# A two-layer hybrid attention trunk: the order of its instructions taken from the scheduler of the language and made by a recorder in the kernel

## The chip, the core and the metric

The kernel runs on one NeuronCore of a Trainium2 chip. Five engines each work through an instruction stream of their own, in order: PE (matmul), DVE (vector), ACT (scalar), POOL and SP, which here issues every DMA. They wait for each other by semaphores. The metric is the device time of one execution in microseconds (us), and the median over several executions is compared.

## What is computed

`x` is (1, 1024, 1024) float32, and two layers are applied to it. In the reference, cut to what matters:

```python
def hybrid_layer(x, ...):
    h = rms_norm(x, g_pre)
    a_q, a_kv, a_g, b_cq, b_ckv, b_kr, c_q, c_kv, z = split_cols(h @ w_in)
    o_a = nsa_attention(...)            # 4 heads: compressed + selected + window 512, sigmoid gates
    o_b = causal_block_attention(...)   # 4 heads: latent attention, rotary key
    o_c = banded_attention(...)         # 8 heads: window 128, with sinks
    mixed = concatenate([o_a, o_b, o_c], -1) * silu(z)
    return x + rms_norm(mixed @ w_out, g_post)
```

With 1024 tokens there are 16 blocks of 64 and the top 16 are selected, so the selected branch is full causal attention. Heads A and C add a bias by distance.

## The kernel before

Tokens are worked in 8 tiles of 128 (`NT`, index `qt`). To keep float32 precision, every operand of a large matmul is held as two float16 parts, high and low: `split` makes them with one ACT copy and one DVE operation, and a product is three float16 matmuls. Each of the two layers has four stretches:

- `first`: norm of `x` (layer 0 only; later norms are in the stretch before), values by token (`by_token`, line 293), keys and queries (`project`, line 286), and the compression of keys (`compress`, `compress_hidden`). `bias_setup` works out the bias rows once, writes them to DRAM, and replicates them there by four DMAs into `bias_rows_a` and eight into `bias_rows_c`.
- swa: `run(swa_units(L), second(L, l), ...)`, the window-128 heads, with the rest of the projections as filler.
- nsa: `run(nsa_units(L), gate_path(L, l), ...)`, the A heads, with the gate columns (`gate_columns`, line 293 for its matmuls) as filler.
- mla: `last_phase`, the B heads, the output product (`product`, line 932), and the norm that starts the next layer.

Attention goes by units (one branch, one or two heads, one `qt`), each in three steps:

- `score`: PE matmuls into a PSUM bank `psS` (lines 639, 654, 679), a DVE operation that adds the bias and takes the row's minimum (`ttr`, line 597), and the exponential on ACT (`expo`, line 600).
- `turn`: the probabilities are split and transposed. Small units do it on PE (line 718, bank `psT`). Units with `by_dma` set (the larger ones of swa and of nsa, and six tiles of the last mla) split into a staging buffer (`sz`, `KC`, `stage_slc`, `stage_win`) and transpose by a DMA that SP issues (`turn_by_dma`, line 167).
- `values`: 64-column PE matmuls with the transposed probabilities into the bank `psO` (line 730).

`mixed` gates and splits a finished tile and transposes it by DMA out of a `ringS` buffer; `product` then multiplies by `w_out`.

`run` writes the steps interleaved by hand, with a lag of 2 units for `turn` and 4 for `values`, and fillers between them:

```python
for i in range(n + lag_v):
    if i < n:
        units[i].score()
    if 0 <= i - lag_t < n:
        units[i - lag_t].turn()
    if 0 <= i - lag_v < n:
        units[i - lag_v].values()
    while more and spent < total * done / whole:
        w = next(filler, None)
```

That is the order in which the program is written. The order on each engine is then made by the scheduler of the language: it takes a tile's slot from a pool with a number of buffers (`bufs`; `ringS` has 3, PSUM has 3 `psS`, 2 `psT`, 1 `psO`, 2 `psJ`), and lists the instructions with a timing model of its own. Weights come in halves into `ringS` (`load_next`), always three loads ahead of their use.

Of the kernel before, what the change touches and what calls it, by code (L numbers as in the profile page):

```python
# [2 lines left out]

# [9 lines left out]
F32 = mybir.dt.float32  # L13
AF = mybir.ActivationFunctionType
# [72 lines left out]
    return (np.arange(128) >= 31).astype(np.float32).reshape(128, 1)  # L87


@with_exitstack  # L90
def trunk(ctx, tc, a, out):
    nc = tc.nc
    pool = ctx.enter_context(tc.tile_pool(name="sb", bufs=1))
    psum = ctx.enter_context(tc.tile_pool(name="ps", bufs=1, space=bass.MemoryType.PSUM))
    uid = [0]
# [16 lines left out]
    BUFS = {"S": 3, "T": 2, "O": 1, "J": 2}  # L112

    def ps(tag):
        uid[0] += 1
        return psum.tile([128, 512], F32, tag=tag, name=f"ps{tag}_{uid[0]}", bufs=BUFS[tag])

    def split(src, scale, hi, lo):
        nc.scalar.activation(hi, src, AF.Copy, scale=scale)  # L119
# [5 lines left out]
    class Ring:  # L125
# [25 lines left out]
    ident = sb([128, 128], F32, "ident")  # L151
    make_identity(nc, ident)
# [627 lines left out]
    def run(units, filler, total, lag_t, lag_v):  # L780

        whole = sum(u.weight for u in units) or 1
        done = spent = 0.0
        more = True
        n = len(units)
# [3 lines that stand above are left out]
                done += units[i].weight  # L789
# [6 lines that stand above are left out]
                more = w is not None  # L796
                spent += w or 0
        for _ in filler:
            pass

    def swa_units(L):
        r = []
        part = sb([128, D], F32, "sz", 2)

        def hl(u):
            return part[:, 256 * (u.h % 4):256 * (u.h % 4) + 512]

        rings = Ring(arena, 2048, 2560), Ring(arena, 4608, 2560), hl
        for hg in (0, 4):
            for qt in range(NT):  # L810
                g = {}
                r.append(Unit(L, "swa", qt, hg, g, None, rings))
                r.append(Unit(L, "swa", qt, hg + 2, g, "swa", rings))
        return r

    def nsa_units(L):
        r = []
        parts = {"slc": [sb([128, D], F32, "sz", 2), sb([128, D], F32, "stage_slc")],
                 "win": [sb([128, D], F32, "KC"), sb([128, 640], F32, "stage_win")]}
# [170 lines left out]
    for l in range(DEPTH):  # L990
        L = Layer()
        L.hT = hT
        first(L, l, wv)
        run(swa_units(L), second(L, l), 80.0, 2, 4)
        third(L, l)
        run(nsa_units(L), gate_path(L, l), 75.0, 2, 4)
        hT, wv = last_phase(L, l, a["x"] if l == 0 else x1_d, x1_d if l < DEPTH - 1 else out)


def lay_out(inp):  # L1000
# [62 lines left out]
```

## Time and profile before

| what | value |
|---|---|
| three timed runs | 1167.44 us median (1163.13 to 1167.81) |
| the profiled execution's own time | 1160.39 us |
| its span in the profile | 1158.5 us |
| mean granted PE clock | 0.973 |
| PE busy | 1010.7 us (87%) |
| DVE, ACT busy | 759.7 us (66%), 706.5 us (61%) |
| DMA queue, share of 16 DMA engines | 64.3% |

The four stretches of layer 0 end at about 117, 240, 435 and 597 us, those of layer 1 at 697, 805, 1000 and 1158 us. In a row of the profile, the idle time is that of the engine just before the rows' instructions, with what ended most of it. "PE busy" counts a matmul until its modelled end, so two matmuls in a row overlap in it.

### The profile page before, as it was taken

The page shows a single profiled execution, that of the slowest core. Times are in us where ns is not written, and L with a number is a line of the kernel's source. Part 1 is how long each engine was busy: PE and PEld are TensorE (multiplying, and loading weights), DVE is VectorE, ACT ScalarE, POOL GpSimd, SP SyncE. Part 2 cuts the span into 40 slices and gives each one's busy share as a digit, 9 for nine tenths or more (in the row PEclk, how much of TensorE's full clock was granted, in tenths as well). Part 3 has the DMA queues.
Part 4 walks back from the last instruction along what each step waited for, and adds up shares of the span by engine and source line. Part 5 has one row for each costly group of instructions (what it writes and reads, how often), then busy time and mean ns, then how long its engine had stood idle before and what let it go on. Part 6 is the DMA issues. An engine that isn't in the chain of part 4 may idle for free.

```text
span 1158.5 us, 25304 instructions
## 1 busy us (share of the span) xinstructions
PE 1010.7 (87%) x9536; PEld 664.0 (57%) x9536; DVE 759.7 (66%) x2268; ACT 706.5 (61%) x1659; POOL 111.0 (10%) x198
## 2 busy tenths in 40 slices
PE   6979898989988877898979989898998887788977
PEld 4634657658776664455646455664776665534443
DVE  6453677756787766687755346876486776756762
ACT  6451676647777677677634246765586666777651
POOL 1000100001111011211000010000011110121010
PEclk9889999999999998999989999999999999989999
DMA  6685476673688695555476435847437877678893
GB/s 241 154 261 138 115 144 117 129 175 100 128 166 162 132 228 157 152 118 129 97 183 203 115 83 120 169 85 178 131 97 145 175 138 134 197 162 196 180 192 98
DMA packets 313499, 174.43 MB, mean 151 GB/s; under 512 B 273580, under 2 KB 289324, under 8 KB 313376
## 3 DMA queue, kind: packets, MB, share of 16 engines
q1 hardware_dynamic: 313376, 172.81, 64.3%
q8 instruction: 75, 1.23, 0.4%
q14 instruction: 48, 0.39, 0.1%
HBM read 76.63 MB, written 21.41 MB: 85 GB/s over the span
## 4 chain that ended last, share of the span: by engine, by line
PE 28%; DMA 16%; DVE 7%; ACT 6%; issue 3%; POOL 1%; SPq 1%; POOLq 0%; ACTq 0%; DVEq 0%
PE psJ L932 9%; PE psJ L286 8%; PE psJ L293 4%; DMA arena<-sz 3%; PE psO L730 3%; PE psS L679 2%; DMA arena<-ringS 2%; DMA V<-ringS 2%; DMA sz<-gate_rows 2%; DVE arena L597 2%; DMA arena<-stage_slc 2%; DMA arena<-stage_win 2%; PE psT L718 2%; ACT arena L600 1%; DVE sz L120 1%
## 5 line engine op out<-in xcount | busy, mean ns | idle before, releaser
L600 ACT ACTIVATE arena<-arena,mx 128x256 f32<-128x256 f32 (+8 forms) x384 | 226.9, 592 | 118.5 <-DVE mx L597 116.1
L293 PE MATMUL psJ<-W,HT 128*128 128x256 f16 x1920 | 241.5, 273 | 0.8 <-DVE VB L120 0.8
L293 PEld LDWEIGHTS <-HT 128*128 128x128 f16 x2304 | 215.2, 99 | 32.0 <-issue 6.6
L286 PE MATMUL psJ<-HT,W 128*128 128x512 f16 x864 | 199.5, 385 | 15.3 <-DVE R L120 7.6
L730 PEld LDWEIGHTS <-arena 128*128 128x128 f16 x2964 | 120.4, 99 | 77.1 <-DMA arena<-sz 20.2
L286 PEld LDWEIGHTS <-W 128*128 128x128 f16 x864 | 84.1, 99 | 110.0 <-issue 10.7
L730 PE MATMUL psO<-V,arena 128*128 128x64 f16 x2304 | 104.4, 194 | 44.7 <-DMA arena<-sz 17.1
L597 DVE CUSTOM_DVE_ANT_0 arena<-psS,R 128x64 f32<-128x64 f32 (+4 forms) x192 | 86.0, 463 | 45.2 <-PE psS L679 19.6
L679 PE MATMUL psS<-KA,QA 128*128 128x512 f16 (+3 forms) x384 | 78.3, 312 | 1.5 <-DVE mx L597 1.2
L120 DVE SCALAR_TENSOR_TENSOR sz<-arena,sz 128x512 f16<-128x512 f32 (+4 forms) x76 | 57.6, 759 | 24.0 <-ACT sz L119 24.0
L600 ACT ACTIVATION_READ_ACCUMULATOR arena<-arena,mx 128x1 f32 x384 | 72.4, 189 | 0.0
L597 DVE CUSTOM_DVE_ANT_0 arena<-psS,arena,nsink 128x256 f32<-128x256 f32 (+1 forms) x128 | 58.4, 460 | 20.5 <-PE psS L654 20.4
L932 PEld LDWEIGHTS <-arena 128*128 128x128 f16 x384 | 37.2, 101 | 56.4 <-DMA arena<-ringS 13.1
L932 PEld LDWEIGHTS <-V 128*128 128x128 f16 x384 | 36.8, 100 | 54.0 <-DMA V<-ringS 11.5
L120 DVE SCALAR_TENSOR_TENSOR arena<-psT,arena 128x128 f16<-128x128 f32 (+3 forms) x144 | 59.6, 429 | 11.3 <-ACT arena L119 10.6
L120 DVE SCALAR_TENSOR_TENSOR W<-ringS,W 128x1024 f16<-128x1024 f32 x48 | 58.3, 1221 | 11.4 <-ACT W L119 10.7
L718 PE MATMUL psT<-ident,arena 128*128 128x128 f32 x300 | 55.8, 286 | 10.8 <-ACT arena L600 9.7
L119 ACT ACTIVATE arena<-psT 128x128 f16<-128x128 f32 (+3 forms) x144 | 51.8, 383 | 20.2 <-PE psT L718 19.6
L171 POOL TENSOR_TENSOR rs<-rs,halfneg 128x1 f32<-128x1 f32 x48 | 26.3, 548 | 384.9 <-DVE rs L170 274.2
L679 PE MATMUL psS<-KB,QB 96*128 96x512 f16 (+3 forms) x288 | 60.5, 337 | 2.5 <-DVE mx L597 2.4
L932 PE MATMUL psJ<-R,arena 128*128 128x512 f16 x192 | 49.8, 414 | 10.5 <-DMA arena<-ringS 10.5
L119 ACT ACTIVATE sz<-arena 128x512 f16<-128x512 f32 (+4 forms) x76 | 51.8, 682 | 9.1 <-DMA arena<-sz 8.0
(156 smaller groups left out, 1644.1 us busy)
## 6 DMA issues: line engine op xcount, KB each, us to landing
ringS<-in_w_in_dram SPq DMA_DIRECT2D x40, 512.0 KB, 4.7
gate_rows<-sz SPq DMA_DIRECT2D x32, 256.0 KB, 3.8
ringS<-in_w_out_dram SPq DMA_DIRECT2D x16, 512.0 KB, 4.4
sz<-gate_rows SPq DMA_DIRECT2D x16, 512.0 KB, 4.7
R<-in_x_dram SPq DMA_DIRECT2D x8, 512.0 KB, 4.1
ringS<-in_cmp_w_dram SPq DMA_DIRECT2D x8, 512.0 KB, 5.3
x<-in_rope_dram SPq DMA_DIRECT2D x8, 512.0 KB, 6.0
x<-in_x_dram SPq DMA_DIRECT2D x8, 512.0 KB, 4.4
```

Source lines behind the costliest of these rows:

```text
L119: nc.scalar.activation(hi, src, AF.Copy, scale=scale)
L120: nc.vector.scalar_tensor_tensor(lo, src, scale, hi, op0=OP.mult, op1=OP.subtract)
L171: nc.gpsimd.tensor_tensor(dst, dst, half_neg[:, :n], op=OP.pow)
L286: nc.tensor.matmul(p, w[:, x, k, sub * 128:(sub + 1) * 128], L.hT[:, y, k, c * 512:(c + 1) * 512], start=(k == 0 and i == 0), stop=(k == K ...
L293: nc.tensor.matmul(p, L.hT[:, y, k, t * 128:(t + 1) * 128], w[:, x, k, :width], start=(k == 0 and i == 0), stop=(k == KT - 1 and i == 2))
L597: nc.vector.tensor_tensor_reduce(o, i0, i1, -alpha, init, OP.add, OP.min, acc)
L600: nc.scalar.activation(b, b, AF.Exp, bias=mx, scale=-1.0, accum_out=sm)
L679: nc.tensor.matmul(p[:, :n], q, k[:, k0 * 128:k1 * 128], start=(i == 0), stop=(i == len(pairs) - 1))
L718: nc.tensor.transpose(p[:, i * 128:(i + 1) * 128], u.b[:, (g + i) * 128:(g + i + 1) * 128], ident)
L730: nc.tensor.matmul(g["O"][:, key * 64:(key + 1) * 64], u.pt[:, x, i, :], v[:, y], start=(key not in seen and j == 0), stop=(last[key] == n ...
L932: nc.tensor.matmul(p, g["mt"][:, x, k], wo[k // 2][:, w, k % 2, cs], start=(k == 0 and i == 0), stop=(k == KT - 1 and i == 2))
```

## The change

The kernel's source up to the end of the layer loop stays as it is, but `nc` in it is now a `Recorder`. Tiles become `Room`s without an address, accesses become `View`s that know which bytes they touch, and each call becomes a `Step` with the set of steps that it must follow. After the loop the kernel makes one fixed tile for every slot, runs a list schedule, and emits the steps in that order inside `tc.manual_schedule()`, which keeps each engine's order as it is emitted. The number of slots of each tag is the one it had. The core of the diff:

```diff
+    def cost(self, s):
+        ...
+        if s.engine == "tensor":
+            n *= 2 if s.name == "transpose" else 4 if src.dtype == F32 else 1
+            return n / 2.4 + 2.2, n / 2.4 + 200.0
+        wake = 35.0
+        if s.engine == "scalar":
+            t = (160.0 if bank else 205.0) + 0.83 * n + (85.0 if s.args[2] == AF.Exp else 0.0)
+            ...
+        if s.engine == "vector":
+            t = 152.0 + 1.045 * n
+            ...
+            return t - 80.0, t + wake
+        ...
+        if s.name == "dma_start_transpose":
+            return 1300.0, (400.0 + size / 220.0, 2000.0)
+        return 520.0, (size / 200.0, 1900.0)
+
+    def schedule(self, slots):
+        ...
+        for s in reversed(self.steps):
+            ...
+            s.key = -tail[s] if s.engine == "sync" else s.n
+        ...
+        while True:
+            for e, heap in ready.items():
+                if heap and free[e] <= now:
+                    _, _, s = heapq.heappop(heap)
+                    order.append(s)
+                    ...
+                    busy, seen = self.cost(s)
+                    if e == "scalar" and s.args[2] not in (AF.Copy, AF.Square, table[0]):
+                        table[0] = s.args[2]
+                        busy, seen = busy + 1283.0, seen + 1283.0
+                    if e == "sync":
+                        bus[0] = max(bus[0], now + busy) + seen[0]
+                        seen = bus[0] + seen[1] - now
...
 def trunk(ctx, tc, a, out):
-    nc = tc.nc
+    nc = Recorder(tc.nc)
...
     def sb(shape, dtype, tag, bufs=1):
-        uid[0] += 1
-        return pool.tile(shape, dtype, tag=tag, name=f"{tag}_{uid[0]}", bufs=bufs)
+        assert count.setdefault(tag, bufs) == bufs
+        words = math.prod(shape[1:]) * (4 if dtype == F32 else 2) // 4
+        return nc.room(tag, words).view(shape, dtype)
...
+    for tag, words in slots.items():
+        home, n = (psum, BUFS[tag[2:]]) if tag[:2] == "ps" and tag[2:] in BUFS else (pool, count[tag])
+        slots[tag] = [home.tile([128, words], F32, tag=f"{tag}_{i}", name=f"{tag}_{i}", bufs=1) for i in range(n)]
+    order = nc.schedule(slots)
+    with tc.manual_schedule():
+        nc.emit(order)
```

`cost` gives for a step, in ns, how long its engine is taken and when its result is seen. On every engine the earliest written step that is ready goes first (`s.n`); only on SP the step with the longest chain behind it goes first (`tail`). All DMAs share one modelled bus. Instructions are neither added nor taken away, but for the loads of ACT's tables: 39 before and 35 now.

Three places show how instructions move. In the changed kernel all rows carry the line of the emitter (359), and names are those of slots. The first place is PE in the nsa stretch of layer 1, at the selected-branch unit of tile 6 (three score matmul rows shown: two of `psS` are its second bank, of 384 columns). `QA` are queries, `KA` keys, `V` values, `W` gate weights, `HT` the transposed norm. Before:

```order
L679 MATMUL psS_12431<-KA_8037,QA_10009 128x512
L679 LDWEIGHTS QA_10009
L679 MATMUL psS_12434<-KA_8037,QA_10009 128x384
L679 LDWEIGHTS QA_10009
L679 MATMUL psS_12434<-KA_8037,QA_10009 128x384
L730 LDWEIGHTS arena_61
L730 MATMUL psO_12272<-V_7730,arena_61 128x64
```

The same scores of the same unit now:

```order
L359 MATMUL psS_88<-KA_90,QA_126 128x512
L359 LDWEIGHTS QA_126
L359 MATMUL psS_87<-KA_90,QA_126 128x384
L359 LDWEIGHTS QA_126
L359 MATMUL psS_87<-KA_90,QA_126 128x384
L359 LDWEIGHTS HT_71
L359 MATMUL psJ_96<-W_97,HT_71 128x256
```

Behind the scores stood values of an earlier unit (15 matmuls), and now stand four matmuls of gate columns, with those values later. Counted on to this unit's own first values matmul, 122 matmuls stood between before (48 of them of 256 columns, gate columns), and 244 stand between now (96 of 256 columns). The second place is SP's stream where the bias rows are replicated and the compression weights (`cmp_w1`, shown as `in_cmp_w_dram`) are loaded, in layer 0. Before:

```order
L123 DMA ringS_315<-in_cmp_w_dram 128x1024
L123 DMA bias_rows<-arena_61 12x1024
L123 DMA bias_rows<-arena_61 12x733
L123 DMA bias_rows_a<-bias_rows 128x1406 x4
L123 DMA bias_rows_c<-bias_rows 128x383 x8
L123 DMA ringS_548<-in_cmp_w_dram 128x1024
L123 DMA ringS_552<-in_cmp_w_dram 128x1024
```

And in the changed kernel:

```order
L359 DMA ringS_82<-in_cmp_w_dram 128x1024
L359 DMA ringS_83<-in_cmp_w_dram 128x1024
L359 DMA bias_rows<-arena_66 12x1024
L359 DMA x_73<-in_rope_dram 128x1024
L359 DMA ringS_84<-in_cmp_w_dram 128x1024
L359 DMA ringS_82<-in_cmp_w_dram 128x1024
L359 DMA bias_rows_c<-bias_rows 128x383 x2
```

All four halves of these weights now go ahead of the replication, where three of them stood behind it. The third place is SP's first instructions, the loads of `x` and of the first norm's gain (`in_norm_pre_dram`). Before:

```order
L123 DMA R_8_74<-in_x_dram 128x1024
L123 DMA arena_61<-in_norm_pre_dram 128x1024
L123 DMA R_8_74<-in_x_dram 128x1024
L123 DMA ringS_99<-in_w_v_dram 128x816
L123 DMA R_8_74<-in_x_dram 128x1024
```

And in the changed kernel:

```order
L359 DMA R_0_72<-in_x_dram 128x1024 x4
L359 DMA arena_66<-in_norm_pre_dram 128x1024
L359 DMA ringS_84<-in_w_in_dram 128x1024
L359 DMA arena_66<-in_buckets_dram 33x1024
L359 DMA relT_86<-in_relT_dram 32x12
```

The gain now stands behind four tiles of `x`, where it stood behind one.

More of the change, by code (lines that the diff above doesn't have):

```diff
@@ L1 @@
+import heapq
+import itertools
 import math
+import re
 from contextlib import ExitStack
@@ L87, in row_mask, with __init__, then, __getitem__ @@
     return (np.arange(128) >= 31).astype(np.float32).reshape(128, 1)
+class View:
+    def __init__(self, tile, steps, p, ids, dtype):
+        self.tile, self.steps, self.p, self.ids, self.dtype = tile, steps, p, ids, dtype
+        self.shape = (p[1] - p[0],) + ids.shape
+    def then(self, step, p=None, ids=None, dtype=None):
+        return View(self.tile, self.steps + (step,), p or self.p, self.ids if ids is None else ids, dtype or self.dtype)
+    def __getitem__(self, key):
+        key = key if isinstance(key, tuple) else (key,)
+        a, b, _ = key[0].indices(self.shape[0])
+        return self.then(("__getitem__", (key,), {}), (self.p[0] + a, self.p[0] + b), self.ids[key[1:]])
+    def bitcast(self, dtype):
+        ids = self.ids
+        if dtype != self.dtype:
+            ids = ids[..., ::2] if dtype == F32 else np.stack([ids, ids + 1], axis=-1).reshape(ids.shape[:-1] + (-1,))
+        return self.then(("bitcast", (dtype,), {}), ids=ids, dtype=dtype)
+    def rearrange(self, text, **sizes):
+        left, right = [re.findall(r"\([^)]*\)|\w+", s) for s in text.split("->")]
+        names, shape = [], []
+        for word, n in zip(left[1:], self.ids.shape):
+            group = word.strip("()").split()
+            known = math.prod(sizes[g] for g in group if g in sizes)
+            names += group
+            shape += [sizes[g] if g in sizes else n if len(group) == 1 else n // known for g in group]
+        to = [word.strip("()").split() for word in right[1:]]
+        flat = [names.index(g) for group in to for g in group]
+        ids = self.ids.reshape(shape).transpose(flat)
+        ids = ids.reshape([math.prod(shape[names.index(g)] for g in group) for group in to])
+        return self.then(("rearrange", (text,), sizes), ids=ids)
+    def unsqueeze(self, d):
+        return self.then(("unsqueeze", (d,), {}), ids=np.expand_dims(self.ids, d - 1))
+    def to_broadcast(self, shape):
+        return self.then(("to_broadcast", (shape,), {}), ids=np.broadcast_to(self.ids, shape[1:]))
+    def region(self):
+        if self.tile.bank:
+            return 0, 128, 1
+        bits = np.zeros(self.tile.words, np.uint8)
+        bits[self.ids.reshape(-1) // 2] = 1
+        return self.p[0], self.p[1], int.from_bytes(np.packbits(bits).tobytes(), "big")
+    def real(self):
+        v = self.tile.slot
+        for name, args, kwargs in self.steps:
+            v = getattr(v, name)(*args, **kwargs)
+        return v
@@ new lines, with __init__, view @@
+class Room:
+    def __init__(self, tag, words, bank):
+        self.tag, self.words, self.bank, self.users, self.slot, self.left = tag, words, bank, [], None, 0
+    def view(self, shape, dtype):
+        n = math.prod(shape[1:])
+        v = View(self, (), (0, 128), np.arange(self.words) * 2, F32)
+        v = v[:shape[0], :n if dtype == F32 else n // 2]
+        if dtype != F32:
+            v = v.bitcast(dtype)
+        if len(shape) > 2:
+            names = "abcd"[:len(shape) - 1]
+            v = v.rearrange(f"p ({' '.join(names)}) -> p {' '.join(names)}", **dict(zip(names, shape[1:])))
+        return v
@@ L90, in trunk @@
 @with_exitstack
 def trunk(ctx, tc, a, out):
-    nc = tc.nc
+    nc = Recorder(tc.nc)
     pool = ctx.enter_context(tc.tile_pool(name="sb", bufs=1))
     psum = ctx.enter_context(tc.tile_pool(name="ps", bufs=1, space=bass.MemoryType.PSUM))
-    uid = [0]
+    count = {}
     def sb(shape, dtype, tag, bufs=1):
-        uid[0] += 1
-        return pool.tile(shape, dtype, tag=tag, name=f"{tag}_{uid[0]}", bufs=bufs)
+        assert count.setdefault(tag, bufs) == bufs
+        words = math.prod(shape[1:]) * (4 if dtype == F32 else 2) // 4
+        return nc.room(tag, words).view(shape, dtype)
@@ L114, in ps @@
     def ps(tag):
-        uid[0] += 1
-        return psum.tile([128, 512], F32, tag=tag, name=f"ps{tag}_{uid[0]}", bufs=BUFS[tag])
+        return nc.room("ps" + tag, 512, bank=True).view([128, 512], F32)
     def split(src, scale, hi, lo):
@@ L148, in trunk @@
     HL = ((0, 0), (0, 1), (1, 0))
-    ident = sb([128, 128], F32, "ident")
-    make_identity(nc, ident)
+    ident = pool.tile([128, 128], F32, tag="ident", name="ident", bufs=1)
+    make_identity(tc.nc, ident)
     half_neg = sb([128, 8], F32, "halfneg")
@@ L997, in trunk @@
         hT, wv = last_phase(L, l, a["x"] if l == 0 else x1_d, x1_d if l < DEPTH - 1 else out)
+    slots = {}
+    for r in nc.rooms:
+        slots[r.tag] = max(slots.get(r.tag, 0), r.words)
+    for tag, words in slots.items():
[4 more added lines that the diff above has]
+        nc.emit(order)
 def lay_out(inp):
```

141 lines of the change are left out of this document (added).

## The prediction

> **What bounds the kernel now.** I read the page first, then busy time by stretch, then the groups of PE's instructions with what they waited for, and at last the order of time around the waits.
>
> ```profile
> span 1158.5 us, 25304 instructions
> PE 1010.7 (87%) x9536; PEld 664.0 (57%) x9536; DVE 759.7 (66%) x2268; ACT 706.5 (61%) x1659; POOL 111.0 (10%) x198
> ```
>
> PE is busiest, and still idle for 148 us (1158.5 less 1010.7). No other engine is near full, so the time is PE's work plus what PE waits for. By stretch (columns: stretch, busy time of each engine, granted clock, share of the DMA engines, GB/s):
>
> ```profile
> 0.00:117.00 117.00, 97.26 (x614) 55.85 (x615) 56.41 (x106) 51.24 (x90) 5.09 (x14) 0.94 0.68 197
> 117.00:240.00 123.00, 112.61 (x1115) 77.43 (x1114) 94.12 (x324) 86.26 (x259) 8.76 (x16) 1.00 0.63 131
> 240.00:435.00 195.00, 171.42 (x2081) 133.09 (x2079) 136.83 (x455) 130.80 (x339) 23.62 (x50) 0.99 0.71 155
> 435.00:597.00 162.00, 142.37 (x1061) 78.78 (x1059) 112.37 (x288) 104.42 (x182) 21.18 (x28) 0.94 0.55 137
> 597.00:697.00 100.00, 90.11 (x762) 57.51 (x760) 49.94 (x119) 41.88 (x94) 4.93 (x9) 1.00 0.49 137
> 697.00:805.00 108.00, 97.92 (x900) 64.37 (x898) 82.32 (x278) 73.20 (x217) 4.93 (x9) 1.00 0.63 135
> 805.00:1000.00 195.00, 168.26 (x2046) 130.27 (x2046) 132.18 (x439) 128.03 (x332) 24.04 (x50) 0.99 0.69 143
> 1000.00:1158.00 158.00, 130.70 (x971) 66.67 (x968) 95.55 (x263) 90.68 (x151) 18.43 (x22) 0.94 0.72 168
> ```
>
> PE's idle time is spread: 20, 10, 24, 20, 10, 10, 27 and 27 us. So there is no single hole to close; what matters is which waits repeat. The groups of PE that waited most (busy, mean ns | idle before, by releaser):
>
> ```profile
> L730 PE MATMUL psO<-V,arena 128*128 128x64 f16 x2304 | 104.4, 194 | 44.7 <-DMA arena<-sz 17.1 <-DMA arena<-stage_slc 13.6 <-DMA arena<-stage_win 10.2
> L286 PE MATMUL psJ<-HT,W 128*128 128x512 f16 x864 | 199.5, 385 | 15.3 <-DVE R L120 7.6 <-DVE tmp L335 5.3 <-ACT hid L384 1.4
> L718 PE MATMUL psT<-ident,arena 128*128 128x128 f32 x300 | 55.8, 286 | 10.8 <-ACT arena L600 9.7 <-DVE arena L120 0.8
> L932 PE MATMUL psJ<-R,arena 128*128 128x512 f16 x192 | 49.8, 414 | 10.5 <-DMA arena<-ringS 10.5
> L932 PE MATMUL psJ<-R,V 128*128 128x512 f16 x192 | 46.7, 395 | 8.5 <-DMA V<-ringS 8.4
> L654 PE MATMUL psS<-KC,QC 128*128 128x256 f16 x224 | 42.3, 272 | 6.9 <-DVE mx L597 4.6 <-DVE QC L748 1.9
> ```
>
> The first row is the largest: 44.7 us in which PE stands at values matmuls whose transposing DMA has not landed. The other five hold 52.0 us together.
>
> **The change, part by part.** No computation is added or taken away; only places in the streams change.
>
> *A. Values later (nsa).* The unit of the first place shown above, in the order of time:
>
> ```profile
> 934.62 0.92 PE L679 MATMUL psS<-KA,QA 128*128 128x512 f16 x4
> 935.51 0.61 PE L730 MATMUL psO<-V,arena 128*128 128x64 f16 x15
> 935.96 2.79 PE L293 MATMUL psJ<-W,HT 128*128 128x256 f16 x24
> ...
> 936.71 0.48 DVE L597 CUSTOM_DVE_ANT_0 arena<-psS,R,mx 128x256 f32<-128x256 f32 x1
> 938.31 1.04 ACT L600 ACTIVATE arena<-arena,mx 128x896 f32<-128x896 f32 x1 [2.62 <-DVE mx L597]
> 939.62 0.94 ACT L119 ACTIVATE stage_slc<-arena 128x896 f16<-128x896 f32 x1
> 940.93 1.09 DVE L120 SCALAR_TENSOR_TENSOR stage_slc<-arena,stage_slc 128x896 f16<-128x896 f32 x1
> 942.10 2.65 SPq L167 DMA_TRANSPOSE arena<-stage_slc  x1
> 947.38 0.79 PE L730 MATMUL psO<-V,arena 128*128 128x64 f16 x21 [2.02 <-DMA arena<-stage_slc]
> ```
>
> The chain from the last score to the landed transpose takes 947.38 − 935.51 = 11.9 us. The 122 matmuls that PE had to do meanwhile covered 9.9 us of it (all but this wait of 2.0). Now 244 stand there, in a similar mix (48 of 256 columns became 96), so the cover is about 9.9 × 244 / 122 = 19.8 us, 7.9 us more than the chain needs. Over the 80 DMA-transposed nsa units the matmul columns that stand between grow 1.8-fold on average, counted in the order. I expect nine tenths of the 44.7 us to go: −40. Ends: −45, and −15 if the chain grows with the pace (first rival). The waits one by one (total, times, longest):
>
> ```profile
> PE psO L730 <- DMA arena<-sz: 17.1, 16, 3.1
> PE psO L730 <- DMA arena<-stage_slc: 13.6, 12, 2.3
> PE psO L730 <- DMA arena<-stage_win: 10.2, 10, 2.6
> ```
>
> *A'. The tail of each ended wait.* A stall also shows as busy time: the last matmul before it counts its full latency.
>
> ```profile
> 983.79 0.87 PE psO L730 x24
> 949.36 2.62 PE psJ L293 x24
> ```
>
> A 64-column matmul in a row costs 0.87/24 = 36 ns, and the group's mean is 194 ns, so each stall hides some 0.16 us. With the 38 waits above that is −6, between 0 and −7.
>
> *B. The start.* SP's second place:
>
> ```profile
> 42.82 12.18 SPq L123 DMA_DIRECT2D bias_rows_c<-bias_rows  x8
> ...
> 57.59 2.06 SPq L123 DMA_DIRECT2D ringS<-in_cmp_w_dram  x2
> ...
> 65.06 1.06 ACT L119 ACTIVATE arena<-ringS 128x1024 f16<-128x1024 f32 x1 [6.66 <-DMA ringS<-in_cmp_w_dram]
> ...
> 69.72 6.84 PE L286 MATMUL psJ<-HT,W 128*128 128x512 f16 x24 [7.43 <-DVE R L120]
> ```
>
> Eight replications hold SP for 12.2 us, the compression weights go out behind them, ACT waits 6.7 us for them, and the splits that free PE's banks come behind ACT's: PE stands 7.4 us. With the weights ahead that wait goes: −7, and the next thing late is the weights of the group behind, which I leave at nothing since they too go out earlier than the last replications. Against it stands the third place: the norm's gain behind three more tiles of `x`.
>
> ```profile
> R<-in_x_dram SPq DMA_DIRECT2D x8, 512.0 KB, 4.1
> ```
>
> Three more tiles are 1.57 MB; at the 197 GB/s of the first stretch this is 8 us later for the first norm. But the four tiles are then there, and DVE and ACT are half idle in that stretch (56 and 51 of 117 us), so part is caught up: +3, between 0 and +8. Together −4.
>
> *C. The clock.* Behind a long stop of PE the granted clock is halved for a while:
>
> ```profile
> 60.00:75.00 15.00, 7.57 (x29) 2.98 (x28) 7.41 (x12) 7.26 (x12) 0.00 (x0) 0.77 0.85 263
> 441.00:452.00 11.00, 7.91 (x30) 3.16 (x31) 7.06 (x23) 8.53 (x13) 1.95 (x2) 0.53 0.79 229
> ```
>
> In the first, 0.23 × 15 = 3.5 us of clock are lost, about half of them while PE works; that stop is B's, so −2. The second belongs to the entry into mla, which I leave. The nsa stretches run at 0.99 in spite of A's waits, so A brings nothing here. The Trainium skill ("TensorE: Matmul & The Clock Gate", Part 1) says that it takes about 3.4 us of idle array to fall to half clock; the trace agrees, since the longest of A's waits is 3.1 us and its stretches keep the clock, and by that rule too C stays small.
>
> *D. Products (L932), 19.0 us.* In the order as many matmuls stand between the last values of a tile and its first product as before, in most places; in the last layer two products are split and interleaved with values. I take 0, between −10 and +12.
>
> *E. Transposes on PE (L718), 10.8 us.* They wait for exponentials, some of them behind a load of ACT's table. The loads go from 39 to 35: −3, between 0 and −10.
>
> *F. The rest.* Scores waiting for a free bank (L654) and like short waits come from DVE being late by under 1 us; about half of such waits can be filled: −5, between 0 and −10.
>
> Sum: −40 − 6 − 4 − 2 + 0 − 3 − 5 = −60. Against the profiled execution's own 1160.4 us this is 1100. That execution lies 7 us under the median of the timed runs (1167.4) and below the fastest of them (1163.1), so for a median I add half of that: 1103.
>
> **The rivals.**
>
> *The DMA queue becomes the bound of nsa.* Where the DMA transposes are dense:
>
> ```profile
> 319.00:435.00 116.00, 97.95 (x1291) 78.06 (x1288) 86.47 (x274) 82.46 (x179) 14.90 (x29) 1.00 0.83 173
> 870.00:1015.00 145.00, 115.94 (x1481) 89.43 (x1478) 103.64 (x330) 98.28 (x213) 18.23 (x34) 0.99 0.78 158
> HBM read 76.63 MB, written 21.41 MB: 85 GB/s over the span
> ```
>
> The DMA engines work 0.83 × 116 = 96 us and 0.78 × 145 = 113 us there. If PE ran without a wait (98 and 116 us), their share would be 0.98 and 0.97, and transposes would queue. For it speaks that share; against it, that the cover has 7.9 us to spare. If only a third of A and A' comes, it is 1103 + 31 = 1134. The Trainium skill ("Perfetto Trace Analysis", Identifying the Most-Contended Engine) calls occupancy of the 16 DMA engines misleading and would judge by HBM utilization instead, whose row here, 85 GB/s, is far from the 358 GB/s that it gives for a core; by that rule this rival would have half its chance. No run yet tells which measure holds for transposes inside SBUF.
>
> *The waits move to the next engine.* With values later, scores run further ahead, and PE could stop at `psS` banks that DVE has not emptied; DVE works 137 of 195 us in nsa. For it: L654 already waits for `mx L597`. Against it: DVE has 58 us free there. Then A is only exchanged: 1160 to 1165.
>
> *Slower: SP falls behind its plan.* The order is fixed with 0.52 us of SP for a copy and 1.3 us for a transpose; the row at 42.82 has 1.52 us for each copy (12.18/8), and that at 942.10 has 2.65 us for one transpose. All DMAs queue in SP's order, so each such excess delays all behind it. It decides when SP is more than 7.9 us behind in nsa, where A's cover ends: then the 44.7 us of waits return, and what stands next in SP's fixed order (gate columns' stores, weights) comes late as well, at the bounds of D and B (+12 and +8): 1160 + 20 = 1180. Against it: an nsa stretch has 40 transposes and some 95 copies, which even at 2.65 and 0.52 us are 155 of 195 us.
>
> *More than the waits named.* The order also differs in hundreds of short places. If all of A, A', D, E and F, the bound of B and 5 us of clock are won: 1160 − 45 − 7 − 19 − 11 − 10 − 7 − 5 = 1056.
>
> **How the numbers follow.** My forecast has 0.50; the DMA queue as a bound 0.20; more than the waits named 0.15; the exchange 0.08; SP behind 0.07. The predicted time is that of the first, 1103. Its own range, by the ends of the terms, is about 1080 to 1125. The range for 8 in 10 takes in most of the second and the fourth: 1052 to 1148, and leaves out the exchange and the slower case. What a measurement of this kernel tells from no change is about 0.5% (6 us). Faster holds the first three cases and none of the others, 0.85; the exchange is mostly within 0.5%: 0.06 same; slower 0.09.
>
> **What would show it.** In the changed kernel's profile the idle time of PE at `psO<-V,arena` should be under 10 us (A); PE's idle time in 0 to 117 should have lost the stop behind the first key projections, and compression weights should go out ahead of the replications (B); the clock should be at least 0.975 (C); L932's group, by its tiles `psJ<-R,arena` and `psJ<-R,V`, should still wait about 19 us (D); DMA share in nsa should rise towards 0.8. The prediction is wrong if values still wait for DMAs, if SP's own waits in nsa grow beyond 8 us at a time, or if PE's new idle time is released by DVE at `psS`.

## The result

The changed kernel takes 1092.93 us (median of 4 runs, 1087.09 to 1093.58) against 1167.37 us of the kernel before on the same chip: a ratio of 0.936, 95% interval 0.932 to 0.940. The prediction was 1103 us, range 1052 to 1148.

The page of the changed kernel begins so (own time 1093.32 us):

```profile
span 1091.5 us, 25293 instructions
PE 998.0 (91%) x9536; PEld 669.3 (61%) x9536; DVE 760.5 (70%) x2268; ACT 691.0 (63%) x1655; POOL 117.2 (11%) x198
```

The span is 67.0 us shorter. PE's idle time went from 147.8 to 93.5 us (-54.3), its busy time from 1010.7 to 998.0 us (-12.7). The two tables below cut the span at the same places of the work in both kernels: PE's first swa, nsa and mla scores of each layer (columns as in the prediction's table by stretch). First the kernel before, then the changed one:

```profile
0.00:117.00 117.00, 97.26 (x614) 55.85 (x615) 56.41 (x106) 51.24 (x90) 5.09 (x14) 0.94 0.68 197
117.00:239.70 122.70, 112.31 (x1109) 77.13 (x1108) 94.12 (x324) 85.96 (x259) 8.76 (x16) 1.00 0.63 130
239.70:413.70 174.00, 154.53 (x1869) 118.96 (x1866) 122.53 (x414) 114.34 (x305) 19.56 (x42) 0.99 0.68 143
413.70:678.40 264.70, 235.02 (x1828) 137.65 (x1825) 163.81 (x397) 150.05 (x266) 26.34 (x38) 0.96 0.57 149
678.40:802.80 124.40, 112.09 (x1108) 77.07 (x1107) 94.09 (x324) 85.87 (x259) 8.76 (x16) 1.00 0.60 129
802.80:980.40 177.60, 154.81 (x1870) 119.05 (x1867) 122.37 (x413) 114.02 (x305) 19.11 (x42) 0.99 0.68 139
980.40:1158.50 178.10, 144.64 (x1162) 78.25 (x1157) 106.39 (x290) 105.03 (x177) 23.36 (x30) 0.94 0.74 171
```

```profile
0.00:114.60 114.60, 97.14 (x614) 56.13 (x615) 56.82 (x106) 50.59 (x90) 5.09 (x14) 0.99 0.66 201
114.60:226.60 112.00, 106.87 (x1079) 75.60 (x1078) 91.18 (x312) 80.75 (x254) 8.73 (x16) 1.00 0.70 138
226.60:385.50 158.90, 151.97 (x1844) 119.73 (x1843) 121.73 (x427) 112.90 (x308) 19.67 (x42) 0.98 0.78 156
385.50:632.20 246.70, 233.23 (x1880) 140.38 (x1876) 165.65 (x399) 147.25 (x265) 28.91 (x38) 0.97 0.64 162
632.20:744.30 112.10, 106.78 (x1079) 75.51 (x1078) 91.11 (x312) 80.84 (x254) 8.73 (x16) 1.00 0.66 136
744.30:904.00 159.70, 151.65 (x1844) 119.99 (x1843) 121.54 (x426) 112.10 (x309) 19.65 (x42) 0.98 0.78 156
904.00:1091.50 187.50, 150.32 (x1213) 81.99 (x1209) 112.53 (x292) 106.56 (x180) 26.41 (x30) 0.90 0.73 166
```

Every stretch is shorter (-2.4, -10.7, -15.1, -18.0, -12.3, -17.9 us) but the last (+9.4), whose clock is 0.90. The matmul counts (behind PE's busy time, the first in a row) show that stretches hand work on: each swa holds 30 matmuls fewer than before, each nsa some 25 fewer and each mla some 50 more, so a stretch's gain is not exact.

All instructions now carry the line of the emitter, so groups are found by their tiles. The groups of PE that answer to those of the prediction, and two that grew; the last row is all waits of scores for a bank (total, times, longest):

```profile
L359 PE MATMUL psO<-V,arena 128*128 128x64 f16 x2304 | 103.2, 193 | 6.7 <-DMA arena<-sz 5.3 <-DMA arena<-stage_slc 1.1
L359 PE MATMUL psJ<-HT,W 128*128 128x512 f16 x864 | 199.9, 388 | 9.5 <-DVE tmp L359 6.2 <-ACT W L359 1.6 <-DVE V L359 0.8
L359 PE MATMUL psT<-ident,arena 128*128 128x128 f32 x300 | 59.5, 290 | 7.1 <-DVE arena L359 3.9 <-ACT arena L359 3.1
L359 PE MATMUL psJ<-R,arena 128*128 128x512 f16 x192 | 48.7, 407 | 2.4 <-DMA arena<-ringS 2.4
L359 PE MATMUL psJ<-R,V 128*128 128x512 f16 x192 | 47.8, 398 | 8.9 <-DMA V<-ringS 8.9
L359 PE MATMUL psS<-KB,QB 96*128 96x512 f16 x144 | 41.1, 397 | 9.6 <-DVE mx L359 9.4
L359 PE MATMUL psT<-ident,x 128*128 128x128 f32 x32 | 6.1, 353 | 11.3 <-DVE x L359 11.3
PE psS L359 <- DVE mx L359: 16.6, 20, 3.8
```

The values (`psO<-V,arena`) lost 38.0 of their 44.7 us of idle time. What grew are mla scores that wait for a bank (`psS<-KB,QB`, 1.9 before; all scores together 16.6 us, 8.3 before) and the very first transposes (8.6 us before).

The unit that the prediction followed, last score to first values, in the changed kernel (PE, DVE, ACT and SP rows of the order of time):

```profile
867.03 0.97 PE L359 MATMUL psS<-KA,QA 128*128 128x512 f16 x3
870.42 0.35 DVE L359 CUSTOM_DVE_ANT_0 arena<-psS,R,mx 128x128 f32<-128x128 f32 x1
870.87 1.04 ACT L359 ACTIVATE arena<-arena,mx 128x896 f32<-128x896 f32 x1 [1.45 <-DVE mx L359]
876.34 0.94 ACT L359 ACTIVATE stage_slc<-arena 128x896 f16<-128x896 f32 x1
877.83 1.09 DVE L359 SCALAR_TENSOR_TENSOR stage_slc<-arena,stage_slc 128x896 f16<-128x896 f32 x1
878.99 1.53 SPq L359 DMA_TRANSPOSE arena<-stage_slc  x1
886.87 0.78 PE L359 MATMUL psO<-V,arena 128*128 128x64 f16 x21
```

The values start 18.9 us after the last score (the end of the first row, 868.00) and wait for nothing; before it was 11.9 us, with a wait of 2.0. But the chain is longer too: the split on ACT starts 4.4 us after the exponential, behind work of other units, where before it followed at once.

### The profile page after: what moved, and what is told of

Read it like the earlier page. It is cut to its first block, busy times and chain, and to the rows that moved or that the text cites. A ratio compares the mean times of both kernels' runs of the same rounds, so it can differ in the third digit from the quotient of the medians.

```text
span 1091.5 us, 25293 instructions
## 1 busy us (share of the span) xinstructions
PE 998.0 (91%) x9536; PEld 669.3 (61%) x9536; DVE 760.5 (70%) x2268; ACT 691.0 (63%) x1655; POOL 117.2 (11%) x198
## 5 line engine op out<-in xcount | busy, mean ns | idle before, releaser
L359 PEld LDWEIGHTS <-HT 128*128 128x128 f16 x3084 | 252.1, 99 | 44.0 <-issue 11.0
L359 PE MATMUL psJ<-W,HT 128*128 128x256 f16 (+1 forms) x2304 | 270.9, 264 | 2.0 <-ACT sz L359 1.8
L359 PEld LDWEIGHTS <-arena 128*128 128x128 f16 x3540 | 169.2, 99 | 80.8 <-issue 11.1
L359 ACT ACTIVATE sz<-psJ 128x256 f32<-128x256 f32 (+1 forms) x92 | 40.4, 440 | 83.0 <-PE psJ L359 55.9
L359 POOL TENSOR_TENSOR rs<-rs,halfneg 128x1 f32<-128x1 f32 x64 | 35.0, 548 | 529.1 <-DVE rs L359 513.5
L359 PE MATMUL psS<-KA,QA 128*128 128x512 f16 (+3 forms) x384 | 82.5, 313 | 0.1
L359 PE MATMUL psS<-KB,QB 96*128 96x512 f16 (+3 forms) x288 | 64.2, 346 | 12.3 <-DVE mx L359 11.9
L359 DVE SCALAR_TENSOR_TENSOR arena<-psT,arena 128x128 f16<-128x128 f32 (+3 forms) x144 | 60.3, 430 | 11.8 <-ACT arena L359 11.3
L359 PE MATMUL psT<-ident,arena 128*128 128x128 f32 x300 | 59.5, 290 | 7.1 <-DVE arena L359 3.9
L359 DVE SCALAR_TENSOR_TENSOR W<-ringS,W 128x1024 f16<-128x1024 f32 x48 | 58.4, 1223 | 10.5 <-ACT W L359 10.3
L359 PE MATMUL psJ<-R,arena 128*128 128x65 f16 (+1 forms) x384 | 55.2, 300 | 2.4 <-DMA arena<-ringS 2.4
L359 ACT ACTIVATE psJ<-psJ 128x512 f32<-128x512 f32 x32 | 18.6, 582 | 59.4 <-DVE tmp L359 59.4
```

The source lines that it names most:

```text
L359: getattr(getattr(self.nc, s.engine), s.name)(*[real(v) for v in s.args], **{k: real(v) for k, v in s.kwargs.items()})
```

## Experiments

Ratios are to the kernel before on the same chip (its median moved from 1160 to 1167 us between sessions). In the table, "left" is the mean over the 80 DMA-transposed nsa units, worked out from each trace, of the time between the end of SP's issue of the transpose and the first values, less the group's idle time divided by 80; it is the time that PE's other work gives a transpose to land.

| kernel | ratio (95%) | idle at psO<-V,arena | split, us | score to issued | score to values | left |
|---|---|---|---|---|---|---|
| before | 1 | 44.7 | 2.6 | 8.1 | 11.0 | 2.4 |
| changed | 0.936 (0.932-0.940) | 6.7 | 4.4 | 11.0 | 15.7 | 4.6 |
| e1, landing unknown to the planner | 1.026 (1.022-1.029) | 75.2 | 3.9 | 9.1 | 12.1 | 2.1 |
| e3, new order in nsa alone | 0.962 (0.957-0.966) | 18.3 | 4.3 | 10.8 | 15.1 | 4.0 |
| e4, by hand, lag 5 | 0.983 (0.979-0.987) | 22.1 | 2.4 | 8.3 | 11.7 | 3.2 |
| e11, landing planned too late | 0.971 (0.968-0.973) | 2.9 | 6.2 | 13.3 | 19.2 | 5.9 |

In these six the column "left" orders the idle time: 2.1, 2.4, 3.2, 4.0, 4.6, 5.9 us go with 75, 45, 22, 18, 7 and 3 us. In the other eight, worked out in the same way, the order is looser: e6 (below) has 3.2 us and waits 39.7 us, e10 has 3.6 and 43.6, e8 has 5.0 and 10.1. So the mean says only roughly how much is waited. "Split" is the time from the exponential's end to the split's end.

**e1: the planner does not know that a transpose lands late.**

```diff
-            return 1300.0, (400.0 + size / 220.0, 2000.0)
+            return 1300.0, (0.0, 0.0)
```

> The planner of the changed kernel with one line altered: it takes a DMA transpose as landed at once (landing time 0 in place of 400 ns + size/220 + 2000 ns). By the planner's own matmul durations the work between a nsa unit's last score and its first values, mean of the 80 DMA-transposed units, falls from 14.7 us to 8.2 us, which is what the kernel before had (8.2 us). Cover theory: PE's idle time at psO<-V,arena returns to 35-50 us (6.7 in the changed kernel, 44.7 before) and the time to 1125-1145. Rival 'the gain is the machinery and the other places' (fixed slots, SP's order): the time stays under 1108.

Measured: 1190.5 us, 1.026, worse than expected by either theory. The groups of values and products:

```profile
L359 PE MATMUL psO<-V,arena 128*128 128x64 f16 x2304 | 108.7, 198 | 75.2 <-DMA arena<-sz 35.5 <-DMA arena<-stage_slc 21.6 <-DMA arena<-stage_win 10.9
L359 PE MATMUL psJ<-R,arena 128*128 128x512 f16 x192 | 52.2, 429 | 16.7 <-DMA arena<-ringS 16.7
L359 PE MATMUL psJ<-R,V 128*128 128x512 f16 x192 | 50.7, 419 | 21.4 <-DMA V<-ringS 21.4
```

The waits are back, and more than before: the planner's splits come later (3.9 us against 2.6 in the kernel before), so the transposes are issued 1 us later behind the score, and PE's other work leaves only 2.1 us for the landing (2.4 before). The products, whose transposes the planner takes as landed at once too, wait 38.1 us (11.3 in the changed kernel). The mean clock is 0.946. So what the change wins hangs on this number of its model; without it, list schedule, slots and SP's order leave the kernel slower than before.

**e2, e3, e5, e6: orders from a table.** In the recorder's schedule the key of a step is its place in a table for its engine, and an engine takes only the next one; accesses are told apart by 16 bits in place of 32, since the old order needs it. For the mixed tables, what is left of the steps at the first scores of a stretch goes on in the other kernel's order, on all engines.

```diff
+ORDER = (
...
-            s.key = -tail[s] if s.engine == "sync" else s.n
+        turn = {e: 0 for e in ready}
+        for e, ns in listed(ready).items():
+            for i, n in enumerate(ns):
+                self.steps[n].key = i
...
-                if heap and free[e] <= now:
+                if heap and free[e] <= now and heap[0][0] == turn[e]:
+                    turn[e] += 1
```

> The changed kernel's recorder, fixed slots and emission, but every engine is given the order of the kernel before, from a table. Order theory: it is the kernel before again, 1167 within 1% (1155 to 1179), idle at psO<-V,arena 40-50 us. Rival 'slots fixed by the kernel or fewer semaphores gain by themselves': 1110 to 1150.

Measured: 1154.8 us, 0.9955 (0.993 to 0.998). With the old order the recorder gives the old time to half a per cent; values wait as before:

```profile
L453 PE MATMUL psO<-V,arena 128*128 128x64 f16 x2304 | 105.5, 195 | 43.3 <-DMA arena<-sz 18.2 <-DMA arena<-stage_slc 11.1 <-DMA arena<-stage_win 8.3
```

The gain is the order, not the fixed slots; the next three are compared with this 0.9955.

> From tables as in the kernel with the old order: old order everywhere, but from the first scores of nsa to the first scores of mla, in both layers, what is left goes in the changed kernel's order on all engines. Cover theory: idle at psO<-V,arena falls below 12 us, and with the stalls' tails the time to 1118-1132 (1167 less 36 to 49). Rival 'the gain lies in all stretches alike': nsa is a third of the span, a third of the 74 us, 1138-1148. Rival 'SP's order by chains is what counts, and it needs the stretches before': over 1150.

Measured: 1117.9 us, 0.9615, 39 us less than e2 by the ratios (0.034 of 1160; 37 by the two medians).

```profile
PE 1000.7 (90%) x9536; PEld 666.3 (60%) x9536; DVE 756.8 (68%) x2268; ACT 703.4 (63%) x1659; POOL 111.7 (10%) x198
L456 PE MATMUL psO<-V,arena 128*128 128x64 f16 x2304 | 102.6, 193 | 18.3 <-DMA arena<-stage_slc 6.9 <-DMA arena<-sz 4.6 <-DMA arena<-stage_win 4.6
```

The cover theory holds: nsa's order alone brings more than half of the gain. The idle time at values fell by 25 us, less than expected (18.3 is not under 12), but PE's busy time fell by 15.0 us as well (1015.7 in e2), so that the time came out at the low end of what was expected.

> From tables: the changed kernel's order up to the first nsa scores of each layer (start, projections, swa), the old order in nsa and mla. The profiles of before and after say what should go in these stretches: PE idle -2.3 and -5.3 us in layer 0, -7.7 and -3.1 us in layer 1, and about 6 us of halved clock in the first stretch. Theory 'the rest beyond nsa lies here': ratio to before 0.974 to 0.985, some 22 us less than the old order from a table (0.9955). Rival 'these stretches only look shorter, since what they save is handed to nsa, which waits for its transposes': ratio 0.988 to 0.997.

Measured: 1136.0 us (1129.8 to 1142.1), 0.970 (0.965 to 0.976): some 29 us less than e2 by the medians, 17 by the two profiled runs. These stretches hold a good part of the gain, as the first theory has it; whether it is more than the 22 us read from the profile, the noise leaves open. The rival's time is out, but what it describes happens in part: in the two profiles the swa stretches are 9.5 and 10.3 us shorter than in e2, and the nsa stretches behind them 2.5 and 10.6 us longer. The start shows no clear gain: up to the first swa scores e5 takes 115.2 us, and the old order takes 115.2 (e6) to 117.4 us (e4). Values wait as in e2 (43.6 us).

> From tables: old order up to mla of each layer, the changed kernel's order in mla. By the profiles idle changes there by -8 and +5 us, and the halved clock by -2 and +8 us of stretch. Theory: no gain in sum, ratio 0.990 to 1.000, with the products' wait down by 4 to 10 us and the entries into mla slower. Rival 'the products' shorter wait is a gain of its own': 0.980 to 0.988.

Measured: 1155.4 us, 0.988 (0.984 to 0.992): 8 us less than e2, at the border of both expectations, so it decides nothing between them. The profile shows an exchange: products wait 10.5 us in place of 19.8 (10.9 and 8.9 in e2), scores wait for banks 18.3 in place of 7.4.

```profile
PE psS L456 <- DVE mx L456: 18.3, 30, 3.7
L456 PE MATMUL psJ<-R,V 128*128 128x512 f16 x192 | 48.9, 405 | 9.0 <-DMA V<-ringS 9.0
L456 PE MATMUL psJ<-R,arena 128*128 128x512 f16 x192 | 48.4, 405 | 1.5 <-DMA arena<-ringS 1.5
```

The three parts sum to -39, -29 and -8 us, 76 together; the changed kernel lies 69 us under e2 (0.9955 less 0.936). With some 5 us of uncertainty in each, the parts add up by the ratios.

**e4: the values later by hand.** The kernel before on the language's scheduler:

```diff
-        run(nsa_units(L), gate_path(L, l), 75.0, 2, 4)
+        run(nsa_units(L), gate_path(L, l), 75.0, 2, 5)
```

> The kernel before, by hand, on the language's scheduler: values of nsa five units behind the scores in place of four, nothing else. The work between last score and first values grows from 8.2 to 9.7 us only (mean of 80, by the planner's durations of matmuls). Cover theory: 38 waits share 44.7 us, 1.2 us each and 3.1 at most; 1.5 us more cover ends about two thirds of them: idle at psO<-V,arena 10-20 us, time 1133-1148. Rival 'the language's scheduler moves the waits to psS or to the ring of turned tiles': 1160-1170.

Measured: 1139.5 us, 0.983 (0.979 to 0.987), idle at values 22.1 us: the time is as the cover theory has it, the idle time a little over its 10 to 20. It is the cleanest test of the cause, with no other machinery changed, and one number brings 20 of the 74 us.

```profile
L730 PE MATMUL psO<-V,arena 128*128 128x64 f16 x2304 | 104.9, 194 | 22.1 <-DMA arena<-sz 11.0 <-DMA arena<-stage_slc 7.5 <-DMA arena<-stage_win 1.6
```

**e7: SP in the order of the program.**

```diff
-            s.key = -tail[s] if s.engine == "sync" else s.n
+            s.key = s.n
```

> The changed kernel, but SP takes the earliest written ready DMA instead of that with the longest chain. The cover in nsa stays (14.9 us in place of 14.7, by the planner's matmul durations). Cover theory: the stop of 7 us behind the first key projections returns (compression weights behind the bias replications again), psO<-V,arena stays under 12 us: ratio 0.940 to 0.952 (the changed kernel has 0.936). Rival 'SP's order by chains carries a large part': above 0.960.

Measured: 1113.6 us, 0.953 (0.949 to 0.957): 20 us slower than the changed kernel, between the two expectations, and not for the reason given. The stop behind the first key projections did not return; the four halves of the compression weights still go out ahead of all replications (the last at 51.31, the first replication at 53.39 us). In the plan their slots are free early enough for that without the order by chains; this is the likely reason and was not traced:

```profile
51.31 0.33 SPq L359 DMA_DIRECT2D ringS<-in_cmp_w_dram  x1
54.04 2.68 SPq L359 DMA_DIRECT2D bias_rows_c<-bias_rows  x4
53.92 21.00 PE L359 MATMUL psJ<-HT,W 128*128 128x512 f16 x96
PE psS L359 <- DVE mx L359: 25.7, 27, 9.8
```

The 20 us are spread: by the marks of the stretches +5.0 us at the start, +10.6 between the first mla scores and layer 1's swa, +3 and +4 in the nsa stretches, -3 at the end. Values wait 6.6 us, as in the changed kernel: cover and SP's order are two gains.

**e8: filler later.** Steps of five functions are ranked otherwise in the planner (a step's `rank` is its number plus a shift for its engine):

```diff
+    @shifted(tensor=400, scalar=150)
     def gate_columns(L, w, g, t, zs):
+        @shifted(tensor=210)
         def product(qt, q):
+        @shifted(scalar=150)
         def score(u):
+        @shifted(tensor=-35)
         def turn(u):
+        @shifted(tensor=-25)
         def values(u):
```

> The changed kernel with five functions' steps ranked otherwise in the planner: gate columns 400 steps later on PE and 150 on ACT, products 210 later on PE, turns 35 and values 25 steps earlier on PE, exponentials 150 later on ACT. Filler is then kept for the moments in which attention has nothing ready. Waits that it could fill in the changed kernel: psS<-DVE mx 16.6, psO<-DVE sz 6.2, psT<-DVE arena 3.9, L932's group 11.3, psO<-V,arena 6.7 us, and 10 to 25 us of halved clock at the entries into mla. Theory 'what is left are holes at stage changes which filler can fill': ratio 0.915 to 0.930. Rival 'held-back filler delays what needs it (gate columns' stores, sz slots, the next norm)': 0.936 to 0.950.

Measured: 1091.3 us, 0.9335 (0.930 to 0.937): not to be told from the changed kernel, and neither of the two expectations. Between the same marks nsa is 6.8 and 8.2 us shorter than in the changed kernel (152.1 and 151.5 us), but swa is 3.6 and 3.7 us longer and the stretch from mla into layer 1 11.2 us longer: the gate columns held back in nsa (some 70 matmuls fewer there) are done behind it.

**e9: matmuls that compute nothing, to hold the clock.**

```diff
+            if busy_pe and left_pe and shut[0] and free["tensor"] <= now and not ready["tensor"] and not self.warm(now, busy_pe):
+                s = Step(-1, "tensor", "matmul", idle, {"start": True, "stop": True})
+                order.append(s)
```

> The changed kernel, whose planner also adds matmuls that compute nothing: where PE has nothing ready and was busy for under 0.75 of the last 3.41 us, it puts a 128-column matmul of a constant into 128 columns of the values' bank that nothing reads (990 of them stand in the order, most of them around 90, 225, 400, 545, 745, 930 and 1020 to 1060 us). In the profile of the changed kernel the clock falls behind a stretch of 3.41 us in which PE was busy for 0.00 to 0.56 of it, the longest single stop in them only 0.8 to 1.4 us at the two entries into mla, and returns only behind one that was 0.83 to 1.00 busy; PE's work in the halved stretches sums to some 50 us, so 25 us are lost. Clock theory: mean clock from 0.968 to 0.985 or more, ratio 0.916 to 0.930 (the changed kernel has 0.936). Rival 'only a stop of over 3.4 us counts, and these stretches have another cause': clock stays at 0.96-0.97, ratio 0.935-0.945. Rival 'the added matmuls delay the real ones': clock rises, ratio 0.936 or more.

Measured: 1099.9 us, 0.946 (0.942 to 0.950), mean clock 0.994. The profile has 1115 added matmuls, not 990. The clock does what the clock theory says, but the time does not: it is slower than the changed kernel, by 0.010 or some 11 us by the ratios (7 us by the medians of two sessions), the third expectation. The same 24 us at the entry into the last mla, in the changed kernel and in e9:

```profile
930.00:954.00 24.00, 12.81 (x84) 6.04 (x84) 15.94 (x45) 19.64 (x33) 5.09 (x8) 0.64 0.56 118
930.00:954.00 24.00, 19.38 (x283) 15.44 (x281) 16.35 (x55) 18.66 (x33) 4.89 (x7) 1.00 0.53 145
```

ACT works 19.6 and 18.7 of 24 us and DVE 15.9 and 16.4: at the entry PE mostly waits for what they make, at whatever clock. The whole last stretch took 188.3 us with a clock of 0.99, and 187.5 with 0.90. That a halved clock costs little here is the likely reading, but it is not shown alone: the added matmuls also take PE's time, and what they delay was not measured apart from what the clock wins.

**e10: flat durations.**

```diff
+        if s.engine == "tensor":
+            return 100.0, 300.0
+        if s.engine != "sync":
+            return 500.0, 600.0
+        return 1000.0, (500.0, 2000.0)
```

> The changed kernel's planner without durations as traced: 100 ns (seen after 300) for every PE step, 500 (600) for DVE, ACT and POOL, 1000 ns, 500 on the bus and 2000 landing for every DMA. By the real matmul durations the mean work between last score and first values in nsa is then 7.2 us (14.7 in the changed kernel, 8.2 in the kernel before). Theory 'the durations make the gain': psO<-V,arena waits 60 us or more, clock under 0.955, ratio 1.015 to 1.06. Rival 'the list schedule by itself makes it (SP by chains, one plan for all engines)': 0.95 to 0.98.

Measured: 1287.8 us, 1.107 (1.104 to 1.109), slower than expected; waits at values are 43.6 us, under what was expected, but scores wait 67.1 us for banks:

```profile
PE psS L369 <- DVE mx L369: 67.1, 68, 3.4
```

A list schedule with flat durations is 11% worse than the old order; the durations make the gain, at more places than the cover.

**e11: landing planned too late.**

```diff
-            return 1300.0, (400.0 + size / 220.0, 2000.0)
+            return 1300.0, (400.0 + size / 220.0, 4000.0)
```

> The changed kernel's planner takes 4000 ns in place of 2000 for the landing of a DMA transpose: mean work between last score and first values 18.1 us in place of 14.7, the least of the 80 units 12.4 in place of 9.6. Cover theory: it is already enough, psO<-V,arena falls from 6.7 to under 3 us and no more than that is won: ratio 0.930 to 0.938. Rival 'more cover costs banks and ring room': psS<-DVE mx and psJ waits grow, ratio 0.945 to 0.970.

Measured: 1130.2 us, 0.971 (0.968 to 0.973): the rival's time. Values hardly wait (2.9 us), but PE's idle time is 112.5 us in place of 93.5, and its busy time 1014.4 in place of 998.0. The waits go to the transposes on PE (7.1 us in the changed kernel) more than to the banks that the rival named (16.6):

```profile
L359 PE MATMUL psT<-ident,arena 128*128 128x128 f32 x300 | 61.7, 299 | 15.1 <-DVE arena L359 10.9 <-ACT arena L359 3.9
PE psS L359 <- DVE mx L359: 19.3, 21, 2.9
```

With 0, 2000 and 4000 ns planned beyond the transfer (e1 drops the 400 ns and the transfer too) the kernel takes 1.026, 0.936 and 0.971: of three values the middle one is best. For a tile of 128x896 it plans 1.3 + 0.4 + 1.0 + 2.0 = 4.7 us from issue to landing, where the semaphores' updates in the traces give medians of 3.9 (before) and 4.4 us (changed) for `arena<-stage_slc`.

**e12: late filler, and the norm's gain ahead.**

```diff
+        for s in [s for s in self.steps if s.engine == "sync"][:2]:
+            s.key = s.n - 1e9
```

> The kernel with late filler (0.9335, interval 0.9297 to 0.9373) and one thing more: SP's first two loads, the first tile of x and the norm's gain, go out ahead of the other tiles of x, as in the kernel before. Start theory: PE's first transposes move from 11.3-12.0 us (changed kernel, late filler) to about 8 us, and the first stretch, up to the first swa scores, from 114.8 to 111-112 us: ratio 0.928 to 0.933. Rival 'DVE and ACT catch up what the three tiles cost, as the prediction's +3 of 0 to +8 allows': first transposes at 8 us, the stretch's end at 114-116 as before, ratio 0.933 to 0.938.

Measured: 1095.2 us, 0.939 (0.937 to 0.942), just above both expected. The first transposes come at 7.9 us, but the next ones wait, and the first swa scores start at 118.1 us (114.8 without):

```profile
7.90 1.97 PE L378 MATMUL psT<-ident,x 128*128 128x128 f32 x8 [7.90 <-DVE x L378]
13.73 1.97 PE L378 MATMUL psT<-ident,tmp 128*128 128x128 f32 x8 [3.86 <-DVE rs L378]
```

No version tried beats the changed kernel by more than the measurement can tell.

## Why the prediction was right, step by step

**A, values later, -40:** measured -38.0 us of idle time at `psO<-V,arena`, and e1, e3 and e4 show the cause. The reason was right but for one assumption: the chain did not stay as it was. From the last score to the issued transpose it grew from 8.1 to 11.0 us (mean of 80), and the split waits behind work of other units on ACT (4.4 us in place of 2.6), where the planner lets the earliest written step go first. So the time left for the landing grew by 2.2 us only (2.4 to 4.6), not by the nearly 10 us that the unit's cover gained in the prediction's sum. That was enough, since the 38 waits were 1.2 us each.

**A', tails, -6:** its size stays open. In e3, where nsa's order alone changed, PE's busy time fell by 15.0 us with 25 us of idle time. Part is the clock (0.967 in e2, 0.970 in e3, some 4 us); the rest, some 11 us, would be twice the term. But in e4 22.6 us of idle time at values went and PE's busy time stayed what it was in the kernel before (1011.0 against 1010.7 us), so these runs do not fix the term.

**B, the start, -4:** measured -2.4, with C's -2 for the same stop in it; and this is hardly clear of what the stretch varies between runs in the old order (115.2 to 117.4 us). The wait of 7.4 us went, and the gain behind three tiles did cost 3.3 us at the first transposes, both as predicted. But taking this back wins nothing: in e12 the next transposes waited and the stretch was 3.3 us longer. And the stop does not need SP's order by chains to go, as e7 shows.

**C, the clock, -2 (0.975):** missed: 0.968 (0.966 to 0.971 in four executions). That it fell is not shown: the 0.973 of the profile before lies above those of 38 later executions of that kernel (0.958 to 0.972, median 0.965). In the first stretch it did rise, from 0.94 to 0.99, and in the last it fell from 0.94 to 0.90. The step that failed was to look only for long stops, and to leave the entries into mla as they were; the last section has what the clock follows. It seems to have cost little: e9 brings the clock to 0.994 and no time.

**D, products, 0:** -7.7 us (19.0 to 11.3), inside its bounds, and paid for at the scores of mla (`psS<-KB,QB` 128x512, 1.9 to 9.6 us), as e6 shows again. **E, transposes on PE, -3:** -3.7 (waits for ACT 9.7 to 3.1, for DVE 0.8 to 3.9 us). **F, the rest, -5:** the idle time that A, B, D and E do not hold fell by some 2.5 us, as a sum of larger parts of both signs. Its reason failed: half of the scores' waits for banks should have been filled, and they doubled (8.3 to 16.6 us; the longest of those that F called under 1 us was 1.2).

The sum came out 7 us short (60 against 67, between the profiled executions; the 3 us added for a median were not needed), by errors of which some cancel. A and A' were given 46 us, and nsa's order alone brings 39 (e3). B, E and F, where start and swa lie, were given 12, and those stretches bring 17 to 29 (e5). What the sum lacked is above all swa: no row of the prediction stood for it, since no group there waits long. Its two stretches shortened by 10.7 and 12.3 us; PE's idle time in them, from 10.4 to 5.1 and from 12.3 to 5.3 us, is half of that, and the other half is the 30 matmuls handed on from each.

**The rivals.** The DMA queue did not bind: the share in nsa rose from 0.68 to 0.78 at the same marks, and transposes landed little later. The page's median for `arena<-stage_slc` (5.0 us before, 3.7 now) rests on 2 and 7 of 20 transposes; by the updates of their semaphores, which the traces hold for all of them, the medians from the end of the issue to the landing are 1.9 to 2.2 us before and 2.1 to 2.5 us now for the four buffers. This fits the Trainium skill ("Perfetto Trace Analysis", Identifying the Most-Contended Engine), which calls the occupancy of the DMA engines misleading. The chain did grow with the pace, as that rival said, but on ACT and DVE. The exchange for `psS` banks came, almost all in mla and 8 us large, a fifth of what A won; these waits are now PE's largest (16.6 us), which the prediction had named as a sign against it. With flat durations (e10) they are 67.1 us. SP did not fall behind, by the sign that the prediction named: its longest own waits are 5.5 us between 227 and 395 us and 6.0 between 750 and 935, under the 8 named.

```profile
SPq L359 <- PE psO L359: 26.2, 18, 5.5
SPq L359 <- ACT sz L359: 9.3, 2, 6.0
```

## What to carry to other kernels

Where an engine repeats short waits for the same kind of transfer, compare two times for each: from the producer's last step to the issued transfer, and to the consumer's first step; what is left between must hold the landing, and 2.1 or 4.6 us of it in the mean went with 75 or 7 us of waiting here. A planner does that for all places at once, but it is worth just what its durations are worth (0.936 as traced, 1.107 with flat ones), and more margin than the landing needs is paid in later splits and in waits elsewhere (e11). An order written by hand can have a good part of it for one number (lag 5: 0.983).

## What the hardware showed

The granted clock went by windows of 3.41 us, not by long stops alone. In the changed kernel it was halved only behind a window in which PE was busy for 0.58 of it or less, and it stayed so until a window was some 0.8 to 1.0 busy. The two entries into mla in the changed kernel, each cut into the window ahead, the halved stretch and the window behind:

```profile
402.88:406.29 3.41, 1.74 (x31) 1.24 (x29) 2.73 (x5) 1.57 (x4) 0.00 (x0) 1.00 1.09 249
406.29:419.94 13.65, 10.83 (x76) 6.94 (x76) 9.24 (x38) 10.43 (x21) 2.92 (x5) 0.50 0.61 208
419.94:423.36 3.42, 3.07 (x18) 1.64 (x17) 3.42 (x11) 3.42 (x9) 0.00 (x0) 1.00 1.00 255
931.87:935.28 3.41, 1.97 (x29) 1.29 (x29) 2.62 (x8) 2.21 (x7) 0.00 (x0) 1.00 0.03 7
935.28:952.35 17.07, 8.55 (x36) 3.44 (x36) 11.75 (x30) 13.92 (x23) 2.48 (x3) 0.50 0.67 144
952.35:955.76 3.41, 3.41 (x17) 1.55 (x16) 0.00 (x0) 2.03 (x3) 1.42 (x2) 0.99 1.09 252
```

PE was busy for 0.51 and 0.58 of the windows ahead (1.74 and 1.97 of 3.41 us), and no single stop in them or the window before was longer than 1.4 us. The line is not sharp in these records: windows of 0.47 and 0.54 left the clock whole elsewhere in the same run. Nor is busy time all that counts: in the kernel before, the window from 31.81 us was 0.86 busy and the next one wholly, with float32 transposes and matmuls of 33 rows and 12 columns (`psS<-arena,relT`) filling most of them, and the clock was halved from 35.22 to 42.05 us. The halved stretches are 4 and 5 windows long; in the second PE was busy for half of 17 us, at half clock. The Trainium skill ("TensorE: Matmul & The Clock Gate", Part 1) has the window of 3413 ns, and says that the clock falls after an idle window; here a window that was half busy was enough. The prediction's reading of that rule, that stops of up to 3.1 us are harmless, held within nsa, where PE is busy around them; but the trace before already had the clock halved behind the window from 1008.02 us, 0.54 busy (1.85 of 3.41 us) with no stop over 1.3 us.
